# GpSimd makes the larger low part of the row operands at the beginning of the up and of the down pass, and it is made first

## Chip, core and metric

One core of a Trainium2 chip runs the whole program. The metric is the device time in microseconds, as the median of several runs; smaller is better. The engines are TensorE (PE, with its weight loads as PEld), VectorE (DVE), ScalarE (ACT), GpSimd (POOL) and the DMA queues of SP, ACT and POOL.

## The reference, cut to what matters

One step of a decoder layer for 512 prompt rows and 64 sample rows (576 rows of 2048 channels): a combined input projection, attention and a convolution branch, an output projection, then the part that matters here, an MLP with a squared ReLU, and a gated embedding:

```python
x = x + jnp.concatenate([attn, conv_y], axis=-1) @ w_out
hid = jnp.square(jax.nn.relu(rms_norm(x, g_mlp) @ w_up))     # 2048 -> 8192
x = x + hid @ w_down                                         # 8192 -> 2048
gate = jax.nn.sigmoid(rms_norm(x, g_ple) @ w_ple_gate)
x = x + (pe @ w_ple) * gate                                  # then a last rms_norm
```

## The kernel before, in words

**Precision.** All matmuls run on a rounded form of float32. A number is split into a high part (the rounded copy, made by ACT in `split_hi`, line L149) and a low part (the difference, made by DVE in `split_lo`, L152), and a product takes three matmuls: high x high (L1547), high x low (L1548), low x high (L1549).

**Tiles of the up and the down pass.** The 576 rows are two halves of 288, the channels pairs of 128-blocks. A pair of input blocks against a pair of output blocks is a 2 x 2 block product, done with seven products instead of eight: seven sums of weight blocks (`w2r`, sums in L1770 to L1772, then split into `w2h` and `w2l`) meet seven sums of row blocks. Such a set of seven row blocks, high and low, is a row operand, `xs`: 128 partitions x 2 x 7 x 288. One tile of work on PE is 21 matmuls of 288 columns, three for each of the seven products. Behind the last tile of an output pair the seven results in PSUM are combined by ACT and DVE (L1663 to L1666, L1676 to L1679); the next output pair can take a PSUM bank only when the combination has read it, L1664 first.

**Passes.** The up pass has 32 output pairs over 8 operands (k = 0 to 7), the down pass 8 output pairs over 32 operands, cut in rounds so that operands can come one after the other: the first round takes three operands for the output pairs 0 to 2, then 4, 5, 6, 7 and 8. A gate pass follows.

**Where the operands come from.** The seven sums of rows (three blocks direct, four computed, `T`) are written to DRAM by POOL's queue (`stored`, L1314 to L1316; tiles `ui` for the up pass, `di` for the down pass) and read back by POOL's queue into the low half of a slot of a ring of eight (L1470), when the slot's last reader on PE is through. Then `slot` builds the operand in the place: it takes three of the seven blocks (128 x 864), lets ACT copy the rounded high part into the high half and DVE subtract it in the low half, and then the other four (128 x 1152). Three up operands (k = 0, 1 and 7) are not read back but made directly from the sums (`split7`).

**The seams.** At the beginning of the up pass the last sums have only just been finished, so five operands (k = 2 to 6) are built within some twenty microseconds; at the beginning of the down pass eight slots change their contents while PE works on the first rounds. Later operands come one at a time.

**Order of the work.** Each engine works through its instructions in the order in which this program writes them. `Beside` keeps queues of background work (generators): behind each tile of PE it adds a credit in microseconds for DVE and steps through generators until the credit is used; a generator yields what its step costs DVE (`EL(n)` for n columns), or a negative number to be called again some tiles later. Queue 0 goes first: the sums of finished tiles, and `norm`, the row norm of the up pass: PE sums the squares (L179), DVE computes the inverse root in small steps (L181, L163 to L170, L183, L185), PE spreads it (L189), ACT copies it (L190). The builds of operands are in queue 1; before the tile that needs an operand its build is finished at once (`flush`).

Of the kernel before, what the change touches and what calls it, by code (L numbers as in the profile page):

```python
# [13 lines left out]
ALU = mybir.AluOpType  # L14
# [6 lines left out]
HR = 288  # L21
# [10 lines left out]
RING = 8  # L32
# [47 lines left out]
def f(ap):  # L80
    return ap.bitcast(F32)
# [13 lines left out]
def EL(n):  # L95

    return n / 960.0 + 0.07
# [45 lines left out]
class Kern:  # L143
# [1194 lines left out]
    def phase2(self):  # L1338
# [39 lines left out]
        def unit(i):  # L1378

            while len(units) <= i:  # L1380
                t = self.place([128, 3, 2, NR], F32R, "xs")
                units.extend(t[:, j] for j in range(3))
            return units[i]
# [75 lines left out]
        def mk(g, j):  # L1459

            h = slots[g, j] = Slot()
            if g == 3:
                h.hi, h.lo = unit(2 * j), unit(2 * j + 1)
            else:
                t = self.xslot()
                h.hi, h.lo = t[:, 0], t[:, 1]
            src = (self.up_in, self.down_in, self.x2)[g - 1][j]
            def load():
                bg.flush(fin_of[g - 1, j])
                nc.gpsimd.dma_start(f(h.lo), src)  # L1470

            if g < 3:
                load()

            def build():
                if g == 3:
                    load()
                yield -3 if g == 2 and j >= RING else -2
                if g < 3:
                    yield from self.slot(t)  # L1480
                    return
                for i in range(2):
                    gv = self.g_ple[:, 2 * j + i:2 * j + i + 1]
                    r = f(h.lo[:, i, :])
                    self.split_hi(h.hi[:, i, :], r, scale=gv)
                    nc.vector.scalar_tensor_tensor(h.lo[:, i, :], r, gv, f(h.hi[:, i, :]), ALU.mult, ALU.subtract)  # L1486
                    yield EL(NR)

            h.work = bg.add(1, build())

        quadlist = [(si, k) for si, ks in enumerate(self.orders) for k in ks]
# [11 lines left out]
        for n in range(RING, len(seq)):  # L1503
            g, j = seq[n]
# [11 lines left out]
        for t, (si, k) in enumerate(quadlist):  # L1516
            g, p, *_ = segs[si]
            ks = self.orders[si]
            n, i = len(ks), t - seg0[si]
            if prev:  # L1520
                pg, ppr, c, r, pfinal, pp_ = prev
# [10 lines left out]
            s = slots[min(g, 3), k]  # L1532
            if s.work is not None:
                bg.flush(s.work)
                s = slots[min(g, 3), k]
            bg.spend(W.prep(t + 2))
            hi, lo = W.hl.pop(t)
# [17 lines left out]
            if i == (n - 2 if g < 4 else 5) and not slow:  # L1555
                if g > 1:
                    bg.flush_all(0)
                r = pre[g](p, lastseg[g, p] == si)
# [7 lines left out]
            if i == n - 1:  # L1566
                if g > 1:
                    bg.flush_all(0)
                if slow:
                    r = pre[g](p, lastseg[g, p] == si)  # L1570
# [11 lines left out]
        pg, ppr, c, r, pfinal, p = prev  # L1582
# [61 lines left out]
            self.split_lo(l, src, h)  # L1644
            yield EL(n)

    def slot(self, s):

        hi, lo = s[:, 0], s[:, 1]
        for i, n in ((0, 3), (3, 4)):  # L1650
            r = f(lo[:, i:i + n, :])
            self.split_hi(hi[:, i:i + n, :], r)
            self.split_lo(lo[:, i:i + n, :], r, hi[:, i:i + n, :])
            yield EL(n * HR)

    def combine_head(self, pr):

# [25 lines left out]
class Slot:  # L1683
    hi = lo = work = None
# [214 lines left out]
```

## Time and profile before

| | |
|---|---|
| median of 3 runs | 2740.95 us (2735.22 to 2743.04) |
| the profiled execution | 2746.47 us, its span 2744.7 us, mean granted clock 0.991 |
| up pass on PE begins | 1043 us |
| down pass on PE begins | about 1770 us |
| builds by `slot` | 37, each with 864 and 1152 columns on ACT and on DVE |
| POOL instructions | 906, 511.0 us busy, most of it ahead of the up pass |

In the rows of the profile, a line is that of the kernel file, and a line of a helper such as L152 collects several uses, which the tile names tell apart (`xs` operands, `w2l` weights). A row of a timeline has start, duration, engine, line, operation, tiles and shapes; "x2" merges two neighbours, even of different shapes; square brackets give idle time of the engine before it and what ended it. In a wait row stand the total, the count and the longest.

### The profile page before, as it was taken

What the parts mean: (1) busy time and instruction counts of PE and PEld (TensorE: products, weight loads), DVE (VectorE), ACT (ScalarE), POOL (GpSimd) and SP (SyncE); (2) the same over time, 40 slices, a digit from 0 to 9 for tenths busy, and PEclk for the clock granted to TensorE, in tenths of its full rate; (3) what the DMA queues carried; (4) which work ended last, traced back from release to release, by engine and by line L of the source; (5) the groups of instructions that cost most, each with busy time, mean ns of one, the idle gap of its engine ahead of it and who ended that gap; (6) DMA issues with size and microseconds to landing.
All of it is one profiled execution on the core that took longest, in us unless ns stands there. A gap on an engine that the chain in (4) does not pass through costs nothing.

```text
span 2744.7 us, 56305 instructions
## 1 busy us (share of the span) xinstructions
PE 2670.7 (97%) x21873; PEld 2575.1 (94%) x21873; DVE 2043.5 (74%) x3553; ACT 1152.6 (42%) x1692; POOL 511.0 (19%) x906
## 2 busy tenths in 40 slices
PE   8999999998999999999999999999999999998997
PEld 8999999877889998999999999999999999998997
DVE  5577777645444447888888888898888888887676
ACT  4222232334443224444444444444444444444554
POOL 2188787601000000000000000100000000000110
PEclk9999999999999999999999999999999999999999
DMA  5488888898754454444444444666565656655675
GB/s 197 148 299 289 301 291 290 287 320 285 253 191 151 160 197 156 154 143 138 138 138 140 145 143 138 242 149 172 164 191 149 182 158 173 179 169 179 199 241 175
DMA packets 238382, 536.12 MB, mean 195 GB/s; under 512 B 25537, under 2 KB 26562, under 8 KB 238114
## 3 DMA queue, kind: packets, MB, share of 16 engines
q1 hardware_dynamic: 170978, 327.86, 37.7%
q0 software_dynamic: 33600, 143.70, 16.7%
q10 hardware_dynamic: 33536, 60.96, 6.9%
q8 instruction: 171, 2.80, 0.4%
q14 instruction: 97, 0.79, 0.1%
HBM read 441.47 MB, written 90.96 MB: 194 GB/s over the span
## 4 chain that ended last, share of the span: by engine, by line
PE 49%; issue 5%; DVE 3%; DMA 1%; ACT 1%; POOL 0%; DVEq 0%; ACTq 0%; POOLq 0%
PE P L1548 14%; PE P L1547 14%; PE P L1549 14%; PE P L1615 2%; PE P L1617 2%; PE P L1616 2%; DVE w2l L152 1%; DMA xs<-x 1%; ACT w2h L149 0%; DMA xs<-di 0%; DMA x<-c 0%; DVE w2r L1770 0%; DVE w2r L1771 0%; DVE w2r L1772 0%; DVE xs L1486 0%
## 5 line engine op out<-in xcount | busy, mean ns | idle before, releaser
L1547 PE MATMUL P<-xs,w2h 128*128 128x288 f32 x3584 | 1064.5, 297 | 17.0 <-DVE c L1664 8.0
L1548 PE MATMUL P<-xs,w2h 128*128 128x288 f32 x3584 | 1064.4, 297 | 4.7 <-DVE xs L152 4.7
L1549 PE MATMUL P<-xs,w2l 128*128 128x288 f32 x3584 | 1061.4, 296 | 2.8 <-DVE w2l L152 2.6
L149 ACT ACTIVATE w2h<-w2r 128x896 fp32r<-128x896 f32 (+1 forms) x632 | 556.0, 889 | 723.7 <-PE P L1548 425.6
L152 DVE TENSOR_TENSOR w2l<-w2r,w2h 128x896 fp32r<-128x896 f32 (+1 forms) x632 | 637.9, 1012 | 218.1 <-ACT w2h L149 215.6
L1547 PEld LDWEIGHTS P<-xs,w2h 128*128 128x128 f32 x3584 | 676.8, 189 | 23.6 <-DVE c L1664 11.1
L1548 PEld LDWEIGHTS P<-xs,w2h 128*128 128x128 f32 x3584 | 677.3, 189 | 7.3 <-DVE xs L152 7.0
L1549 PEld LDWEIGHTS P<-xs,w2l 128*128 128x128 f32 x3584 | 674.9, 188 | 5.1 <-DVE w2l L152 4.9
L497 PE MATMUL U<-xh,whi 128*128 128x288 f32 x1792 | 400.6, 305 | 3.6 <-ACT xh L149 2.2
L497 PE MATMUL U<-xh,wlo 128*128 128x288 f32 x1792 | 385.3, 297 | 1.4 <-DVE wlo L129 1.4
L497 PE MATMUL U<-xl,whi 128*128 128x288 f32 x1792 | 385.2, 297 | 1.6 <-DVE xl L331 1.6
L497 PEld LDWEIGHTS U<-xh,whi 128*128 128x128 f32 x1792 | 288.2, 190 | 22.5 <-issue 16.3
L123 ACT ACTIVATE whi<-wraw 128x512 fp32r<-128x512 f32 x224 | 141.2, 630 | 393.5 <-PE U L497 217.7
L497 PEld LDWEIGHTS U<-xl,whi 128*128 128x128 f32 x1792 | 289.8, 190 | 2.6 <-DVE xl L331 2.5
L497 PEld LDWEIGHTS U<-xh,wlo 128*128 128x128 f32 x1792 | 289.7, 190 | 2.2 <-DVE wlo L129 2.1
L129 DVE TENSOR_TENSOR wlo<-wraw,whi 128x512 fp32r<-128x512 f32 x224 | 160.2, 715 | 133.9 <-ACT whi L123 132.5
L1044 DVE SCALAR_TENSOR_TENSOR y<-ue,cv,y 128x512 f32<-128x512 f32 x240 | 183.8, 766 | 5.3
L1770 DVE TENSOR_TENSOR w2r<-w2r 128x512 f32<-128x512 f32 (+1 forms) x273 | 177.7, 651 | 5.2 <-DMA w2r<-in_w_down 5.2
L1045 POOL TENSOR_SCALAR cvt<-us,cv 128x64 f32<-128x64 f32 x240 | 162.8, 678 | 22.3
L1615 PE MATMUL P<-xs,w2h 128*128 128x288 f32 x512 | 151.8, 297 | 0.4 <-ACT c L1663 0.4
L1617 PE MATMUL P<-xs,w2l 128*128 128x288 f32 x512 | 151.0, 295 | 1.1 <-DVE w2l L152 1.0
L1616 PE MATMUL P<-xs,w2h 128*128 128x288 f32 x512 | 150.8, 295 | 0.0
(382 smaller groups left out, 2761.1 us busy)
## 6 DMA issues: line engine op xcount, KB each, us to landing
k<-in_cache_kv SPq DMA_DIRECT2D x256, 256.0 KB, 4.7
v<-in_cache_kv SPq DMA_DIRECT2D x256, 256.0 KB, 4.6
w2r<-in_w_up SPq DMA_DIRECT2D x127, 512.0 KB, 4.0
w2r<-in_w_down SPq DMA_DIRECT2D x112, 512.0 KB, 4.3
wraw<-in_w_main ACTq DMA_DIRECT2D x156, 256.0 KB, 4.9
xs<-di POOLq DMA_DIRECT2D x32, 1008.0 KB, 6.1
w2r<-in_w_gate SPq DMA_DIRECT2D x60, 512.0 KB, 4.6
x<-c POOLq DMA_DIRECT2D x48, 576.0 KB, 6.4
```

Source lines behind the costliest of these rows:

```text
L149: self.nc.scalar.activation(out, in_, AF.Copy, **kw)
L152: self.nc.vector.tensor_tensor(out, in_, f(hi), ALU.subtract)
L497: self.nc.tensor.matmul(u[:, r, :HR], w, x[:, r * HR:(r + 1) * HR], start=first and n == 0, stop=last and n == 2)
L1044: nc.vector.scalar_tensor_tensor(y, ue[:, j:j + NPR], w, y, ALU.mult, ALU.add)
L1045: nc.gpsimd.tensor_scalar(t, us[:, :, j:j + 8], w, None, ALU.mult)
L1547: nc.tensor.matmul(o, hi[:, ia, :], s.hi[:, ib, :], start=(i == 0), stop=False)
L1548: nc.tensor.matmul(o, hi[:, ia, :], s.lo[:, ib, :], start=False, stop=False)
L1549: nc.tensor.matmul(o, lo[:, ia, :], s.hi[:, ib, :], start=False, stop=(i == n - 1))
L1615: nc.tensor.matmul(o, hi[:, ia, :], s.hi[:, kh, rows], start=first and kh == 0, stop=False)
L1616: nc.tensor.matmul(o, hi[:, ia, :], s.lo[:, kh, rows], start=False, stop=False)
L1617: nc.tensor.matmul(o, lo[:, ia, :], s.hi[:, kh, rows], start=False, stop=last and kh == 1)
L1770: lambda: V(w[:, :, 4:6, :], w[:, :, 0:1, :].broadcast_to([128, m, 2, 128]), w[:, :, 1:3, :], ALU.add),
```

## The change

`slot` gets an argument `seam`, which is true for the five up operands that it builds and for the first eight down operands. There the part of four blocks comes ahead of the part of three. ACT makes its high part as before, but its low part is subtracted by GpSimd; and the generator yields once, with the cost of the part of three alone, where it yielded twice. Other operands are built as before. `f` reads a tile as plain float32.

```diff
                 if g < 3:
-                    yield from self.slot(t)
+                    yield from self.slot(t, g == 1 or j < RING)
                     return
...
-    def slot(self, s):
+    def slot(self, s, seam):
 
         hi, lo = s[:, 0], s[:, 1]
-        for i, n in ((0, 3), (3, 4)):
+        for i, n in ((3, 4), (0, 3)) if seam else ((0, 3), (3, 4)):
             r = f(lo[:, i:i + n, :])
             self.split_hi(hi[:, i:i + n, :], r)
-            self.split_lo(lo[:, i:i + n, :], r, hi[:, i:i + n, :])
-            yield EL(n * HR)
+            if seam and i:
+                self.nc.gpsimd.tensor_tensor(lo[:, i:i + n, :], r, f(hi[:, i:i + n, :]), ALU.subtract)
+            else:
+                self.split_lo(lo[:, i:i + n, :], r, hi[:, i:i + n, :])
+                yield EL(n * HR)
```

Three lines are added, so that lines behind it have numbers three higher in the kernel after; GpSimd's subtraction is its L1654.

On DVE at the beginning of the up pass stood, behind the direct build of operand 7 (`acc` are the squares of the rows, `w2r` the weight sums):

```order
L152 TENSOR_TENSOR xs<-xs 128x864
L152 TENSOR_TENSOR xs<-xs 128x1152
L152 TENSOR_TENSOR w2l<-w2r,w2h 128x896
L1290 TENSOR_TENSOR acc_12131<-acc_12131,sq_14258 128x576
L152 TENSOR_TENSOR xs<-xs 128x864
L152 TENSOR_TENSOR xs<-xs 128x1152
L1770 TENSOR_TENSOR w2r<-w2r 128x256
L152 TENSOR_TENSOR w2l<-w2r,w2h 128x896
```

and at the same place stands now, down to the third build and the start of the row norm:

```order
L152 TENSOR_TENSOR xs<-xs 128x864
L152 TENSOR_TENSOR w2l<-w2r,w2h 128x896
L1290 TENSOR_TENSOR acc_12131<-acc_12131,sq_14258 128x576 x2
L152 TENSOR_TENSOR xs<-xs 128x864
L1773 TENSOR_TENSOR w2r<-w2r 128x256
L152 TENSOR_TENSOR w2l<-w2r,w2h 128x896
L1774 TENSOR_TENSOR w2r<-w2r 128x128
L152 TENSOR_TENSOR xs<-xs 128x864
L1775 TENSOR_TENSOR w2r<-w2r 128x128
L152 TENSOR_TENSOR w2l<-w2r,w2h 128x896
L181 TENSOR_SCALAR rrm<-P 128x5
L163 TENSOR_SCALAR rrt<-rrm 128x5
```

The parts of 1152 columns are gone; the second accumulation has come forward, and so has the norm, whose fourteen instructions on DVE (L181 to L185) now stand between the third and the fourth build. Before, they stood behind the twelfth tile of the up pass, now PE's sum for them (L179) stands behind the fifth.

On POOL at the beginning of the down pass stood (`di_116` to `di_120` are the sums for the operands 3 to 7, `x_0` to `x_2` partial results that are added in DRAM, `di_144` the last up tile):

```order
L1470 DMA xs<-di_116 128x2016
L1470 DMA xs<-di_117 128x2016
L1470 DMA xs<-di_118 128x2016
L1470 DMA xs<-di_119 128x2016
L1470 DMA xs<-di_120 128x2016
L1363 DMA x_0_81<-c 128x1152
L1314 DMA di_144<-c 128x288
```

and now:

```order
L1470 DMA xs<-di_116 128x2016
L1654 TENSOR_TENSOR xs<-xs 128x1152
L1470 DMA xs<-di_117 128x2016
L1470 DMA xs<-di_118 128x2016
L1654 TENSOR_TENSOR xs<-xs 128x1152
L1470 DMA xs<-di_119 128x2016
L1470 DMA xs<-di_120 128x2016
L1654 TENSOR_TENSOR xs<-xs 128x1152
L1363 DMA x_0_81<-c 128x1152
L1654 TENSOR_TENSOR xs<-xs 128x1152
L1314 DMA di_144<-c 128x288
```

Loads and stores of POOL's queue now stand behind subtractions; the eight of the down pass are the four shown and four more among the stores that follow. At the up pass the five stand together, behind the last load and ahead of the first store of the pass.

## The prediction

> **What bounds the kernel now.** I read the busy times first, then a table of stretches around the two places where the change acts, the waits of TensorE, and last the timeline of VectorE there. On the page TensorE (PE) is busy almost throughout, so the most that any change can win is the small idle time in it.
>
> ```profile
> PE 2670.7 (97%) x21873; PEld 2575.1 (94%) x21873; DVE 2043.5 (74%) x3553; ACT 1152.6 (42%) x1692; POOL 511.0 (19%) x906
> ```
>
> The table of stretches (length, then busy time of PE, PEld, DVE, ACT and POOL, then the granted clock) cuts out the beginning of the up pass (from 1043 us) and of the down pass (from about 1770 us):
>
> ```profile
> 1050.00:1073.00 23.00, 19.02 (x129) 16.99 (x127) 22.06 (x28) 15.98 (x19) 0.00 (x0) 1.00 0.65 237
> 1073.00:1120.00 47.00, 46.53 (x342) 45.27 (x343) 40.76 (x75) 20.45 (x26) 3.25 (x6) 1.00 0.42 128
> 1740.00:1760.00 20.00, 20.00 (x152) 20.00 (x152) 16.68 (x28) 10.90 (x14) 3.23 (x6) 1.00 0.67 223
> 1760.00:1784.00 24.00, 20.12 (x134) 19.06 (x134) 21.94 (x34) 11.08 (x15) 2.68 (x6) 0.93 0.91 350
> 1784.00:1807.00 23.00, 19.91 (x142) 18.70 (x142) 19.87 (x35) 10.56 (x14) 3.49 (x5) 1.00 0.65 171
> 1807.00:1834.00 27.00, 25.65 (x189) 25.05 (x188) 26.16 (x41) 14.56 (x18) 1.72 (x2) 1.00 0.61 143
> 1834.00:1890.00 56.00, 55.96 (x418) 55.83 (x419) 50.23 (x77) 27.72 (x32) 4.26 (x6) 1.00 0.65 182
> ```
>
> In the first and in the fourth to sixth row PE is idle for 3.98, 3.88, 3.09 and 1.35 us while DVE has hardly any idle time (0.94, 2.06, 3.13 and 0.84 us). Ahead of and behind them PE is full. So VectorE bounds the two seams, and only there. The waits of PE over the whole program name the same engine, by the low parts of the operands (xs) and by the combination that frees a PSUM bank (c):
>
> ```profile
> PE P L1547 <- DVE c L1664: 8.0, 11, 1.3
> PE P L1548 <- DVE xs L152: 4.7, 8, 1.1
> ```
>
> **What the change takes from VectorE.** Thirteen operands are built in the seams, five for the up pass and eight for the down pass. Here are three builds of the up seam in VectorE's timeline, an accumulation and a weight split (w2l) between them, and the combination behind the seam; and the groups of the two forms:
>
> ```profile
> 1050.66 2.42 DVE L152 TENSOR_TENSOR xs<-xs 128x864 fp32r<-128x864 f32 x2 [0.35 <-ACT xs L149]
> 1053.99 0.75 DVE L1290 TENSOR_TENSOR acc<-acc,sq 128x576 f32<-128x576 f32 x1
> 1054.66 2.32 DVE L152 TENSOR_TENSOR xs<-xs 128x864 fp32r<-128x864 f32 x2
> 1064.72 1.08 DVE L152 TENSOR_TENSOR w2l<-w2r,w2h 128x896 fp32r<-128x896 f32 x1
> 1066.06 2.32 DVE L152 TENSOR_TENSOR xs<-xs 128x864 fp32r<-128x864 f32 x2
> 1072.68 0.45 DVE L1664 TENSOR_TENSOR c<-c,P 128x288 f32<-128x288 f32 x1
> L152 DVE TENSOR_TENSOR xs<-xs 128x1152 fp32r<-128x1152 f32 x37 | 50.1, 1355 | 0.0
> L152 DVE TENSOR_TENSOR xs<-xs 128x864 fp32r<-128x864 f32 x37 | 39.0, 1054 | 4.1 <-ACT xs L149 3.9
> ```
>
> A build holds VectorE for 2.32 us; without its larger part 1.05 us are left, so 1.27 us go from each.
>
> **What GpSimd needs for it.** The trace has no subtraction of this size on POOL. It has two smaller ones with two inputs, at moments when VectorE did nothing: 64 columns (shortest, median, longest ns of seven) and 128 columns.
>
> ```profile
> L1056 POOL TENSOR_TENSOR ysum<-ysum,ys x7: 322/323/325, 223.9 to 535.9; 128x64 f32<-128x64 f32 x7
> 62.70 0.46 POOL L663 TENSOR_TENSOR suf<-suf,L 128x128 f32<-128x128 f32 x1
> ```
>
> 64 more columns cost 0.137 us, 2.14 ns each; 1152 columns are 0.46 + 1024 x 0.00214 = 2.65 us, my value. The low bound is VectorE's own 1.27 us; the high one scales with the 0.99 us that the 128 columns take beside a busy VectorE (below), 2.65 x 0.99 / 0.46 = 5.7 us. I stay with the undisturbed pair, since what the high row holds more is waiting, which I count by itself. The Trainium skill (GPSIMD Engine Reference, section 3.1) gives 4497 ns for such an addition of 2048 columns; in proportion that is an estimate of 2.53 us, and the sum below would be 1.4 us smaller by it.
>
> **What POOL does to VectorE meanwhile.** This decides the sign. Two moments of the trace, POOL and DVE side by side:
>
> ```profile
> 58.90 0.17 DVE L168 TENSOR_TENSOR rrt<-rrs 128x5 f32<-128x5 f32 x1
> 58.92 0.47 POOL L663 TENSOR_TENSOR suf<-suf,L 128x128 f32<-128x128 f32 x1
> 59.10 0.31 DVE L169 SCALAR_TENSOR_TENSOR rrt<-rrt,rrm 128x5 f32<-128x5 f32 x1
> 60.54 0.69 DVE L183 TENSOR_TENSOR xraw<-ident,rrs 128x512 f32<-128x512 f32 x1
> 60.56 0.99 POOL L663 TENSOR_TENSOR suf<-suf,L 128x128 f32<-128x128 f32 x1
> ```
>
> The DVE instruction that started at 59.10 does the same tiny work as its neighbour of 0.17 us, but takes 0.31 us and ends at 59.41, just behind the POOL instruction's end at 59.39. In the second pair POOL is the one that waits: its 0.46 us become 0.99, the missing half being VectorE's 0.69. So the two engines exclude each other when both read two tensors from SBUF, in both directions, and each seems to wait for the other's whole instruction. The rows show it for a POOL instruction of 0.46 us only; whether VectorE also stands still for 2.65 us is the open step. The Trainium skill (SBUF — State Buffer, "Who interferes with whom") says so for any length: the second to start fully blocks until the first has finished. If that holds, moving 1.27 us off VectorE closes VectorE for 2.65 us: 1.38 us worse for each operand.
>
> **The up seam, summed on VectorE from 1050.66 to 1072.68.** Removed: 5 x 1.27 = 6.35. Added: 5 x 2.65 = 13.25 of closed time. One accumulation (L1290) moves in from behind the seam: 0.67. And, since the first part no longer counts against the scheduler's credit, the whole norm chain moves in between the third and the fourth build. Its rows in the trace of before:
>
> ```profile
> 1084.61 0.17 DVE L181 TENSOR_SCALAR rrm<-P 128x5 f32<-128x5 f32 x1 [1.56 <-PE P L179]
> 1087.64 0.25 DVE L185 TENSOR_SCALAR dg<-ident,rrs 128x64 f32<-128x64 f32 x1
> ```
>
> It runs 3.2 us from 1084.61 to the end of the second row, behind a wait of 1.56 us for PE. There it stood beside a full PE and cost nothing; in the seam its 3.2 us and half of the wait, 0.8 us, lie on the path. Of the same step, PE's few small matmuls (L179, L189) and ACT's two copies (L190) come earlier too, in a stretch where both wait for VectorE anyway: nothing. VectorE's idle 0.94 us cover as much. Sum: 13.25 - 6.35 + 0.67 + 3.2 + 0.8 - 0.94 = 10.6; the 0.47 us that PE idles from 1073 to 1120, partly at that chain, come back: **+10.1 us**.
>
> **The down seam.** Marks in VectorE's timeline: the first two builds, the second part of the third, the fifth and the sixth, and the combination that frees PE's banks at the start and at the end:
>
> ```profile
> 1760.43 2.32 DVE L152 TENSOR_TENSOR xs<-xs 128x864 fp32r<-128x864 f32 x2
> 1767.61 2.32 DVE L152 TENSOR_TENSOR xs<-xs 128x864 fp32r<-128x864 f32 x2
> 1771.06 0.45 DVE L1664 TENSOR_TENSOR c<-c,P 128x288 f32<-128x288 f32 x1
> 1779.55 1.35 DVE L152 TENSOR_TENSOR xs<-xs 128x1152 fp32r<-128x1152 f32 x1
> 1821.54 2.32 DVE L152 TENSOR_TENSOR xs<-xs 128x864 fp32r<-128x864 f32 x2
> 1829.96 2.32 DVE L152 TENSOR_TENSOR xs<-xs 128x864 fp32r<-128x864 f32 x2
> 1833.54 0.45 DVE L1664 TENSOR_TENSOR c<-c,P 128x288 f32<-128x288 f32 x1
> ```
>
> Between 1760.43 and 1833.54 stood the builds of six operands; in the new order seven POOL parts and the smaller part of the seventh operand fall there. Removed 6 x 1.27 = 7.6; added 7 x 2.65 = 18.55, and 1.05: +12.0. VectorE's idle time there is 6.03 us; I let half of it cover, 3.0, because the rest waits for PE or ACT in places that move along. The combinations read PSUM and one tensor of SBUF, which I take not to be excluded; one POOL part lies beside one, 2.0 us. That leaves **+7.0 us**. The third operand's larger part comes earlier than 1779.55, which is part of the cover, not a further gain. The eighth operand is built where VectorE has 5.8 us to spare in 56: nothing.
>
> Costed at nothing: on POOL, the loads of the down operands 4 to 7 and the stores of the last up tile and of x1 now queue behind POOL parts that wait for ACT; each is one part later, 2.65 us, and the fifth operand is not built before 1821.54, fifty microseconds behind the last up tile. If that cover were gone, 2.65 us would be the price. ACT does the same two copies in the other order.
>
> **Sum.** The profiled execution took 2746.47 us; 2746.5 + 10.1 + 7.0 = 2763.6. The median of the runs, 2740.95, lies 5.5 lower, so **2758 us**.
>
> **Rivals.** *VectorE is not closed for the whole instruction*, only for short pieces of it. For it: no POOL instruction over 0.99 us that reads two tensors is in the trace; against it: 59.41 against 59.39. Then VectorE is 1.27 us lighter per build; up, 3.98 us of idle PE come back less 2.5 for the norm chain, 1.5; down, some 6 of 8.3: 2741 - 7.5 = 2733.5. It decides if VectorE loses less than 1.27 us per part. Chance 0.08, three quarters of it below the bound of faster. *The closed time finds cover*: all of it in the down seam (6.0 us idle and six combinations), and in the up seam the POOL parts cost only what they remove, so that the norm chain and the accumulation remain, about 4: 2745. Against it: 0.94 us of idle time in the up seam. Chance 0.09. *The clock falls as well.* In the down seam, PE idled before these rows,
>
> ```profile
> 1779.41 0.40 PE L1547 MATMUL P<-xs,w2h 128*128 128x288 f32 x1 [1.98 <-ACT xs L149]
> 1781.60 0.44 PE L1547 MATMUL P<-xs,w2h 128*128 128x288 f32 x1
> ```
>
> and the stretch has a clock of 0.93: 24 x 0.07 / 0.5 = 3.4 us at half speed, 1.7 us lost. My stalls are longer than those; four such losses, where VectorE doesn't hide them, give 2758 + 7 = 2765. Chance 0.13.
>
> **The numbers.** A measurement tells 0.3%, 8 us, from no change. Forecast 0.70; slower with the clock 0.83; same 0.09 + 0.02 = 0.11; faster 0.06. The range: down by a POOL part without its fixed share, 1152 x 2.14 ns = 2.47 us (12 x 0.18 = 2.2), the other half of the idle cover (3.0) and half of the norm chain with its wait (2.0), to 2751, and on to 2746, most of the way to the second rival; up by no cover under a combination (2) and four clock losses (7), about 2768. What is left out holds the first rival, the rest of the second and little of the third, some 0.18.
>
> **What would show it.** POOL L1654 near 2.65 us, or over it by a DVE instruction that it waits for; DVE instructions in the seams (w2l at 1.08, xs at 1.05, w2r) two to three times as long, ending just behind a POOL part; the stretch of the up seam some 10 us longer, PE idle there about 14 instead of 4, the down seam 7. I am wrong if w2l keeps 1.08 us beside L1654, or if POOL parts take under 1.5 us.

## The result, and the profile after

The changed kernel takes **2764.19 us** as the median of four runs (2759.30 to 2775.75), the kernel before 2738.09 beside it (four runs, 2728.60 to 2743.04): 1.0086 times as long, 95% interval 1.0064 to 1.0107. The forecast was 2758, range 2746 to 2768. The profiled execution took 2760.86 us (its span 2759.1, mean granted clock 0.984).

The page's busy times of the kernel after:

```profile
PE 2668.7 (97%) x21873; PEld 2575.8 (93%) x21873; DVE 2058.7 (75%) x3540; ACT 1154.0 (42%) x1692; POOL 548.3 (20%) x919
```

VectorE has 13 instructions fewer and is busy 15.2 us longer: what was taken from it came back as waiting inside its instructions. Stretches of the seams (length, busy PE, PEld, DVE, ACT, POOL, then the clock), first of the kernel before, then of the kernel after:

```profile
1040.00:1100.00 60.00, 55.84 (x401) 53.03 (x401) 51.19 (x83) 30.18 (x38) 3.16 (x6) 1.00 0.52 175
1770.00:1834.00 64.00, 55.67 (x387) 52.83 (x386) 58.01 (x96) 30.43 (x39) 5.74 (x8) 0.97 0.68 194
1834.00:1890.00 56.00, 55.96 (x418) 55.83 (x419) 50.23 (x77) 27.72 (x32) 4.26 (x6) 1.00 0.65 182
```

```profile
1040.00:1100.00 60.00, 46.15 (x305) 44.60 (x304) 48.64 (x65) 27.66 (x33) 20.03 (x14) 0.86 0.44 156
1770.00:1834.00 64.00, 52.76 (x342) 51.13 (x342) 58.12 (x86) 28.85 (x37) 17.31 (x14) 0.87 0.64 186
1834.00:1890.00 56.00, 52.62 (x379) 51.69 (x378) 49.57 (x72) 22.80 (x28) 9.38 (x7) 0.97 0.48 119
```

In the same lengths PE does 96, 45 and 39 instructions less, its clock falls to 0.86, 0.87 and 0.97, and POOL is busy 17, 12 and 5 us longer. In the third row of before PE was full; now it idles for 3.4 us. PE's waits for the low parts and for the combination, over the whole program after:

```profile
PE P L1548 <- DVE xs L152: 16.0, 4, 7.6
PE P L1549 <- DVE w2l L152: 8.3, 9, 1.8
PE P L1547 <- DVE c L1667: 7.2, 8, 2.1
PE P L1547 <- ACT c L1666: 4.6, 2, 3.7
```

The wait for `xs` was 4.7 us in eight pieces and is 16.0 us in four; that for `w2l` was 2.6 us in four and is 8.3 in nine. The wait for the combination on VectorE (L1667, L1664 before) did not grow in sum, 7.2 us after 8.0, but its longest did, 2.1 after 1.3, and that on ScalarE (L1666) was 2.0 us in three pieces. GpSimd's subtraction by itself (shortest, median, longest ns):

```profile
L1654 POOL TENSOR_TENSOR xs<-xs x13: 2615/2970/3466, 1049.9 to 1850.7; 128x1152 fp32r<-128x1152 f32 x13
```

The undisturbed ones take 2.62 to 2.65 us, the others up to one VectorE instruction more. The open step of the prediction stands in the timelines of POOL and DVE in the up seam:

```profile
1049.90 2.64 POOL L1654 TENSOR_TENSOR xs<-xs 128x1152 fp32r<-128x1152 f32 x1 [4.19 <-ACT xs L149]
1050.66 2.79 DVE L152 TENSOR_TENSOR xs<-xs 128x864 fp32r<-128x864 f32 x1 [1.40 <-ACT xs L149]
1052.60 3.41 POOL L1654 TENSOR_TENSOR xs<-xs 128x1152 fp32r<-128x1152 f32 x1
1053.38 3.58 DVE L152 TENSOR_TENSOR w2l<-w2r,w2h 128x896 fp32r<-128x896 f32 x1
1055.97 3.47 POOL L1654 TENSOR_TENSOR xs<-xs 128x1152 fp32r<-128x1152 f32 x1
1056.88 3.18 DVE L1290 TENSOR_TENSOR acc<-acc,sq 128x576 f32<-128x576 f32 x1
...
1070.24 0.17 DVE L181 TENSOR_SCALAR rrm<-P 128x5 f32<-128x5 f32 x1 [2.42 <-PE P L179]
1071.22 2.65 POOL L1654 TENSOR_TENSOR xs<-xs 128x1152 fp32r<-128x1152 f32 x1 [8.70 <-ACT xs L149]
1071.26 2.65 DVE L170 SCALAR_TENSOR_TENSOR rrs<-rrt,rrs 128x5 f32<-128x5 f32 x1
```

Read the ends: POOL 1052.54, DVE 1053.45; POOL 1056.01, DVE 1056.96; POOL 1059.44, DVE 1060.06. Each VectorE instruction ends 0.6 to 1.0 us behind a POOL part, which is about its own undisturbed time, and each POOL part ends 2.5 to 2.6 us behind a VectorE instruction. So the two take strict turns, one whole instruction each. A `w2l` that takes 1.08 us alone takes 3.58, and in the last row one of the norm's steps on 128 x 5 numbers lasts 2.65 us instead of 0.17. The Trainium skill (SBUF — State Buffer, "Who interferes with whom") says that the one that comes second is blocked for the whole instruction; these rows agree, at 2.65 us. Two rows of the down seam below do not fit it by their recorded starts; there the measurement decides (last section).

PE in the same seam, at full and at half clock (in brackets the wait ahead of the row):

```profile
1054.01 0.30 PE L1548 MATMUL P<-xs,w2h 128*128 128x288 f32 x1
1054.15 0.30 PE L1549 MATMUL P<-xs,w2l 128*128 128x288 f32 x1
...
1064.16 0.61 PE L1548 MATMUL P<-xs,w2h 128*128 128x288 f32 x1 [7.60 <-DVE xs L152]
1064.57 0.44 PE L1549 MATMUL P<-xs,w2l 128*128 128x288 f32 x1
1064.81 0.44 PE L1547 MATMUL P<-xs,w2h 128*128 128x288 f32 x1
```

Behind the wait of 7.60 us matmuls follow each other every 0.24 us instead of 0.14. The trace's record of the clock has it at half for 10.24 us from 1058.6 and 6.83 us from 1075.7 (before: never in this seam), and in the down seam for four stretches of 20.5 us together (before: one of 3.41).

In the down seam:

```profile
1777.91 0.45 DVE L1680 TENSOR_TENSOR t<-P,t 128x288 f32<-128x288 f32 x1
1777.97 2.68 POOL L1654 TENSOR_TENSOR xs<-xs 128x1152 fp32r<-128x1152 f32 x1 [1.41 <-ACT xs L149]
1778.28 0.45 DVE L1681 TENSOR_TENSOR c<-c,P 128x288 f32<-128x288 f32 x1
1778.76 2.50 DVE L1682 TENSOR_TENSOR c<-c,t 128x576 f32<-128x576 f32 x1
...
1817.58 0.86 POOL L1363 DMA_DIRECT2D x<-c  x1 [5.66 <-DVE c L1682]
1817.80 4.30 DVE L152 TENSOR_TENSOR w2l<-w2r,w2h 128x896 fp32r<-128x896 f32 x1
1818.16 2.98 POOL L1654 TENSOR_TENSOR xs<-xs 128x1152 fp32r<-128x1152 f32 x1
...
1850.27 4.31 DVE L152 TENSOR_TENSOR w2l<-w2r,w2h 128x896 fp32r<-128x896 f32 x1
1850.66 2.97 POOL L1654 TENSOR_TENSOR xs<-xs 128x1152 fp32r<-128x1152 f32 x1
```

The steps of the combination that read PSUM and one tensor of SBUF (L1680, L1681) keep their 0.45 us beside the POOL part, as the prediction assumed. The step behind them (L1682), with both inputs in SBUF, takes 2.50 us; elsewhere in this trace it takes 0.76. The last pair belongs to the eighth operand, which was costed at nothing.

**Where the time went.** To place it I take from each trace the start of every 21st of the 10752 large matmuls of the up and the down pass, that is of each tile, numbered through. "Up seam" is from tile 0 to tile 16, "up pass" from there to tile 240, "down seam" from tile 248 to tile 290.

| us, profiled executions | before | after | difference |
|---|---|---|---|
| up seam | 53.28 | 66.18 | +12.90 |
| up pass behind it (224 tiles) | 628.56 | 619.73 | -8.83 |
| down seam | 130.50 | 143.49 | +12.99 |
| all else | 1932.37 | 1929.70 | -2.67 |
| span | 2744.71 | 2759.10 | +14.39 |

The seams lose 25.9 us. That the two profiled spans differ by 14.4 only is due to the rest, and above all to the up pass: of its 8.8 us, 1.4 lie in the tiles 16 to 29, where PE before still waited for `w2l` and did the norm's last matmuls, and 7.5 are a shorter time for each tile, which is taken up at the end. The medians differ by 26.1 us, with an interval of 17.5 to 29.3, so that their closeness to 25.9 doesn't show whether the other runs of the change had the short tiles too.

### The profile page after: what moved, and what is told of

Same layout as the page of the kernel before. It is cut to its first block, busy times and chain, and to the rows that moved or that the text cites. A ratio compares the mean times of both kernels' runs of the same rounds, so it can differ in the third digit from the quotient of the medians.

```text
span 2759.1 us, 56320 instructions
## 1 busy us (share of the span) xinstructions
PE 2668.7 (97%) x21873; PEld 2575.8 (93%) x21873; DVE 2058.7 (75%) x3540; ACT 1154.0 (42%) x1692; POOL 548.3 (20%) x919
## 5 line engine op out<-in xcount | busy, mean ns | idle before, releaser
L152 DVE TENSOR_TENSOR w2l<-w2r,w2h 128x896 fp32r<-128x896 f32 (+1 forms) x632 | 647.3, 1026 | 214.1 <-ACT w2h L149 212.6
L1548 PEld LDWEIGHTS P<-xs,w2h 128*128 128x128 f32 x3584 | 681.3, 190 | 17.3 <-DVE xs L152 17.1
```

Source lines behind the costliest of these rows:

```text
L152: self.nc.vector.tensor_tensor(out, in_, f(hi), ALU.subtract)
L1548: nc.tensor.matmul(o, hi[:, ia, :], s.lo[:, ib, :], start=False, stop=False)
```

## The experiments

Two theories stood against each other. *Closed*: POOL's reads exclude VectorE, 2.65 us for each part against 1.27 saved. *Order and queue*: what costs is the new order (larger part first, one credit, the norm in the seam) and that the part arrives late from POOL, behind its queue. Each kernel's stretches, as above, with its median and that of the kernel before on the same chip:

| kernel | ratio (95%) | medians | up seam | up pass | down seam |
|---|---|---|---|---|---|
| before | | | 53.28 | 628.56 | 130.50 |
| the change | 1.0086 (1.0064 to 1.0107) | 2764.19 / 2738.09 | 66.18 | 619.73 | 143.49 |
| up_only | 1.0027 (1.0009 to 1.0045) | 2748.87 / 2742.32 | 65.95 | 619.73 | 130.60 |
| down_only | 1.0047 (1.0024 to 1.0069) | 2756.58 / 2742.32 | 53.19 | 628.55 | 144.90 |
| credit_kept | 1.0058 (1.0035 to 1.0081) | 2761.37 / 2742.32 | 60.25 | 628.55 | 144.59 |
| vector_same_order | 1.0007 (0.9991 to 1.0024) | 2745.94 / 2742.32 | 55.82 | 627.20 | 132.12 |
| pool_writes_only | 0.9974 (0.9952 to 0.9996) | 2730.96 / 2738.95 | 55.61 | 619.73 | 125.04 |
| pool_reads_one | 1.0039 (1.0019 to 1.0058) | 2751.04 / 2738.95 | 60.85 | 619.73 | 138.45 |
| pool_pieces | 1.0073 (1.0051 to 1.0096) | 2759.67 / 2738.95 | 62.06 | 619.73 | 148.49 |
| clock_kept | 1.0069 (1.0044 to 1.0095) | 2757.42 / 2738.95 | 62.62 | 619.73 | 143.81 |
| last_two | 1.0026 (1.0001 to 1.0050) | 2744.53 / 2740.72 | 53.26 | 628.56 | 132.87 |
| vector_larger_first | 1.0006 (0.9987 to 1.0025) | 2739.90 / 2740.72 | 53.46 | 621.53 | 131.31 |

The stretches come from one profiled execution each; in those of down_only and vector_same_order 26 and 6 matmul records are missing, so that their figures can be off by 0.2 us. All diffs are against the changed kernel, with most lines around them left out.

**One seam at a time**, up_only and down_only:

```diff
-                    yield from self.slot(t, g == 1 or j < RING)
+                    yield from self.slot(t, g == 1)                    # up_only
+                    yield from self.slot(t, g == 2 and j < RING)       # down_only
```

> The change in the up seam alone. Measured from the first tile of the up pass on PE to the seventeenth, before took 53.3 us and the changed kernel 66.2. Closed VectorE: 66 us here, the down seam (from the 249th to the 291st tile, 130.5 us before, 143.5 changed) as before, the whole 10 to 13 us longer than before (ratio 1.004 to 1.005). If the loss came from POOL's queue (late loads and stores of the down pass), both stretches stay as before and the ratio is 1.000.

> The change in the down seam alone. Closed VectorE: the up stretch 53 us as before, the down stretch 143 us, the whole about 13 us longer (ratio 1.005). If the two seams hang together (one loss, passed on), the down stretch stays near 131 us.

Each seam loses as much alone as in the whole change (up +12.7 of 12.9; down +14.4 against 13.0), and the other one stays as before. The two add up; nothing is carried from one to the other through POOL's queue. The median of down_only is 14.3 us above before, as expected; that of up_only is only 6.5 above, less than the 10 to 13 expected (see the end).

**The work on POOL with the norm where it was**, credit_kept: the part on POOL is counted in the credit too, so that the norm stays behind the twelfth tile.

```diff
                 self.nc.gpsimd.tensor_tensor(lo[:, i:i + n, :], r, f(hi[:, i:i + n, :]), ALU.subtract)
+                yield EL(n * HR)
```

> GpSimd makes the parts as in the change, but the generator also yields for them, with the cost that VectorE's part had, so that the row norm stays where it was (behind the twelfth tile). Closed VectorE: in the up stretch the 5 x (2.65 - 1.27) = 7 us of the parts remain, 60 us; the down stretch 141 to 144 us; the whole +18 to +20 us (ratio 1.007). If the moved norm were the main loss of the up seam, its stretch falls to 54 us.

**The order with the work on VectorE**, vector_same_order: everything as in the change, the subtraction on DVE.

```diff
-                self.nc.gpsimd.tensor_tensor(lo[:, i:i + n, :], r, f(hi[:, i:i + n, :]), ALU.subtract)
+                self.split_lo(lo[:, i:i + n, :], r, hi[:, i:i + n, :])
```

> All as in the change (larger part first, one yield, norm moved forward), but VectorE makes the larger parts itself. Closed VectorE: only the norm and the accumulation remain as a loss in the up seam, 4 to 5 us: 57 to 58 us; the down stretch 128 to 131 us, since the third operand's larger part comes earlier; the whole +1 to +4 us (ratio 1.000 to 1.0015). If the order and the credit were the cause and not GpSimd, both stretches are as long as in the changed kernel, 66 and 143 us.

These two split the up seam. Order and norm alone cost 2.5 us there and 1.6 in the down seam, both about one microsecond beside their bounds (1.4 of the 2.5 come back in the up pass, 627.20 after 628.56). The five POOL parts, with the norm where it was, cost 60.25 - 53.28 = 7.0 us, which is 5 x (2.65 - 1.27) = 6.9. In the down seam they cost 14.1, where 8 x 1.38 is 11.0; that is 0.6 us more than expected. Two pairs of the table differ in nothing but the engine that subtracts: the change and vector_same_order (10.4 us in the up seam, 11.4 in the down seam), and credit_kept and vector_larger_first, the last of the experiments (6.8 and 13.3). So order and credit are not the cause. In the up seam 12.9 is 3.4 us more than 2.5 + 7.0: the norm's steps meet the POOL parts (the row of 2.65 us above). How much of each is shut-out time and how much the clock can't be read from these two: credit_kept too ran at half clock for 10.2 us in its up seam.

**What on POOL does the harm.** Three kernels put other work of about the same length in the part's place: three fills that read nothing (pool_writes_only), two copies that read one tensor (pool_reads_one), and the subtraction in four pieces of 288 columns (pool_pieces). In the first two the low half isn't the difference.

```diff
-                self.nc.gpsimd.tensor_tensor(lo[:, i:i + n, :], r, f(hi[:, i:i + n, :]), ALU.subtract)
+                for _ in range(3):                                                  # pool_writes_only
+                    self.nc.gpsimd.memset(f(lo[:, i:i + n, :]), 0.0)
+                for _ in range(2):                                                  # pool_reads_one
+                    self.nc.gpsimd.tensor_copy(lo[:, i:i + n, :], r)
+                for k in range(i, i + n):                                           # pool_pieces
+                    self.nc.gpsimd.tensor_tensor(lo[:, k, :], f(lo[:, k, :]), f(hi[:, k, :]), ALU.subtract)
```

> In place of the subtraction, GpSimd fills the larger low part with zeros three times (the low part of these blocks is left out of the computation): about as long as the subtraction, three times 1.0 us by the rate of the 2560-column fill, but it reads nothing. If what closes VectorE is the reading by both, VectorE's instructions keep their durations (w2l 1.08 us) and it is 1.27 us lighter per operand: the up stretch 51 to 55 us, the down stretch 126 to 131 us, the whole between 0 and 6 us shorter than before (ratio 0.998 to 1.000). If the loss comes from a part being ready late, from POOL's queue, or from any POOL instruction, the stretches stay near 66 and 143 us.

The fills and VectorE's weight splits in the up seam (1040 to 1120 us), in the groups of pool_writes_only, and one such split beside ten fills in a row, in its timelines:

```profile
L1655 POOL MEMSET xs<- 128x1152 f32 x39 | 42.2, 1087 | 14.7 <-ACT xs L149 13.2
L152 DVE TENSOR_TENSOR w2l<-w2r,w2h 128x896 fp32r<-128x896 f32 x23 | 25.0, 1088 | 6.4 <-ACT w2h L149 6.4
1051.27 10.76 POOL L1655 MEMSET xs<- 128x1152 f32 x10 [4.16 <-ACT xs L149]
1053.03 1.09 DVE L152 TENSOR_TENSOR w2l<-w2r,w2h 128x896 fp32r<-128x896 f32 x1
```

POOL is occupied for 3 x 1.09 = 3.26 us per operand, longer than by the subtraction, and so the low part is ready later, but `w2l` keeps its 1.09 us. So neither POOL's queue nor a late part is the cause. The down seam becomes 5.5 us shorter than before, 1.0 beyond the expected bound: this is what taking 1.27 us per operand off VectorE would bring there if POOL left it alone. The up seam, with the norm in it, was 55.6, 0.6 us beyond its bound. The whole is faster than before, 0.9974 (0.9952 to 0.9996), by 8.0 us, where up to 6 were expected and the two seams give 3.1; in the profiled execution the up pass behind them gives 8.8 more. The Trainium skill (SBUF — State Buffer, "Who interferes with whom") says that a VectorE instruction with two SBUF inputs collides with a GpSimd instruction that reads SBUF and not with one that only writes; these rows agree.

> In place of the subtraction, GpSimd copies the part onto itself twice (one tensor read, the subtraction left out); a copy of 1152 columns should take 1.0 to 1.5 us. If a read of one tensor closes VectorE as well, w2l beside it takes 2 us and more and the stretches lie between those of before and of the change by the length of the copies: 58 to 64 us up, 135 to 142 us down. If only two tensors on both sides collide, as for the zeros: 51 to 55 and 126 to 131 us.

Reads of one tensor close VectorE as well: `w2l` takes 2.03 us, and both seams come out inside the bounds expected for this. In the timeline of pool_reads_one, and its copies over the whole program:

```profile
1055.13 2.03 DVE L152 TENSOR_TENSOR w2l<-w2r,w2h 128x896 fp32r<-128x896 f32 x1
1057.09 3.31 DVE L1290 TENSOR_TENSOR acc<-acc,sq 128x576 f32<-128x576 f32 x2
```

```profile
L1655 POOL CAST xs<-xs x26: 1147/1484/2057, 1053.2 to 1845.8; 128x1152 fp32r<-128x1152 f32 x26
```

> GpSimd makes the larger low part in four instructions of 288 columns, 0.8 us each by the rate of the trace, instead of one of 2.65. Exclusion by whole instructions: no VectorE instruction waits for more than 0.8 to 0.9 us at a time (2.65 and more in the change), VectorE gets one instruction in after each piece, and the closed time grows to 4 x 0.8 = 3.2 us per operand, so that the stretches are as long as in the change or up to 5 us longer (66 to 71 and 143 to 149 us). If the exclusion were by short slices, nothing changes in the single waits beside that in the change.

```profile
L1655 POOL TENSOR_TENSOR xs<-xs x52: 781/982/1709, 1050.5 to 1852.5; 128x288 fp32r<-128x288 f32 x52
```

Four pieces are 4 x 0.78 = 3.1 us undisturbed, 4.3 at their mean of 1.08. Single VectorE instructions wait less, but the down seam is 148.5, longer than with whole parts; the up seam, 62.1, fell below the 66 that I had expected at the least. Smaller pieces do not help the sum of the seams, 26.8 us after 25.9.

**The clock**, clock_kept: 36 matmuls more ahead of tile 4 and 18 ahead of tile 6 of the up pass keep PE at work while it waits for VectorE; their products are added to a result in the up pass.

```diff
+                for _ in range({4: 36, 6: 18}.get(t, 0)):
+                    nc.tensor.matmul(pr[3][:, :HR], last[0][:, 3, :], last[1].hi[:, 1, :], start=False, stop=False)
+                last = hi, s
```

> The changed kernel with PE kept busy in the up seam: 36 matmuls of the tile before are repeated ahead of the fifth tile and 18 ahead of the seventh (they add to one product, whose result is not the reference's), where PE stood idle for 7.8 and 4.0 us and its clock fell to half for 17 us. If the clock costs about 5 us of the up stretch, as the rows after those stalls say (tile 7 starts 2.8 us later than its operand allows), it falls from 66 to 60 to 62 us, with a clock of 1.00 in the table of stretches. If VectorE hides the half clock, the stretch stays at 65 to 67 us. The down stretch stays at 143 us.

The stretch from 1040 to 1110 us, of the change and of clock_kept:

```profile
1040.00:1110.00 70.00, 56.15 (x381) 54.60 (x380) 57.28 (x80) 32.19 (x39) 20.03 (x14) 0.88 0.46 159
```

```profile
1040.00:1110.00 70.00, 65.04 (x462) 63.82 (x461) 59.24 (x84) 33.08 (x40) 20.17 (x14) 0.95 0.48 164
```

The clock rises from 0.88 to 0.95, not to the expected 1.00 (half for 6.8 us instead of 17.1), and the up seam shrinks from 66.18 to 62.62, 0.6 us above its bound: the lower clock costs **3.6 us** of the up seam, and I take it to be more, since some of it was left. The norm's wait for PE falls with it, from 2.42 to 1.02 us. The down seam is as in the change.

**The end of the down seam**, last_two: only the seventh and the eighth operand of the down pass go to POOL, the ones that I had costed at least.

```diff
-                    yield from self.slot(t, g == 1 or j < RING)
+                    yield from self.slot(t, g == 2 and j in (6, 7))
```

> The change for the seventh and the eighth operand of the down pass alone, all others as before; there PE was full before and VectorE had 5.8 us to spare in 56. If spare time on average is cover, as the prediction had it for the eighth operand, the down stretch stays at 130 to 131 us and the ratio at 1.000. If a closed VectorE costs at once what it delays, because the low parts of the weights are made only two tiles ahead of their use, each part costs PE 1 to 3 us: 133 to 136 us (ratio 1.001 to 1.002).

The timelines around the eighth operand's part, and the wait of PE from 1820 to 1920 us:

```profile
1853.54 4.29 DVE L152 TENSOR_TENSOR w2l<-w2r,w2h 128x896 fp32r<-128x896 f32 x1
1853.92 2.95 POOL L1654 TENSOR_TENSOR xs<-xs 128x1152 fp32r<-128x1152 f32 x1
```

```profile
PE P L1549 <- DVE w2l L152: 2.2, 1, 2.2
```

The seventh costs nothing. The eighth makes the down seam 2.4 us longer, nearly all of it in one wait of 2.2 us, between the two stretches that were expected: the instruction that POOL shut out is a weight split that PE needs at once. So VectorE's 5.8 us of idle time in that stretch were no cover.

**A version for use**, vector_larger_first: the new order of the two parts, both on VectorE, both counted.

```diff
-                self.nc.gpsimd.tensor_tensor(lo[:, i:i + n, :], r, f(hi[:, i:i + n, :]), ALU.subtract)
+                self.split_lo(lo[:, i:i + n, :], r, hi[:, i:i + n, :])
+                yield EL(n * HR)
```

> VectorE makes both parts as before, with both yields, but the larger part first: what is left of the change without GpSimd and without the moved norm. It could beat both kernels if the third down operand's larger part, which comes late before (1779.55), was worth its stall of some 4 us: the down stretch 127 to 130 us, the up stretch 53 us, ratio 0.998 to 1.000. If what counts there is VectorE's total work, both stretches stay within a microsecond of before (53.3 and 130.5 us), ratio 1.000.

Both stretches stay within a microsecond of before, the second of the two expectations, and the whole can't be told from the kernel before. No version that computes the reference was shown to be faster than that.

## Why the prediction was right, and where it was wrong

- **Direction and size.** Slower, 2764 against a forecast of 2758: in the range. The sum was +17.1 us; the seams and the medians say 26. It was 9 us too small; that the forecast missed by 6 only is luck, since the median of the kernel before is now 2.9 us below the one that it started from. The range held because its upper end had room for the two terms that fell short, the cover and the clock.
- **What POOL needs.** 2.65 us from the two small shapes; measured 2.62 to 2.65 undisturbed. The Trainium skill's figure (GPSIMD Engine Reference, section 3.1), in proportion an estimate of 2.53, is 0.1 us low.
- **The open step.** VectorE is closed for the whole instruction: shown by the turns in the timeline and by pool_writes_only, where POOL is as occupied but reads nothing. That kernel is the first rival's world: its down seam is 5.5 us shorter, where the rival had some 6; its up seam is 2.3 longer, where the rival had 1.5 less.
- **PSUM.** Combinations that read PSUM and one SBUF tensor are not excluded: right. But the cover that was built on it was too large, since the step L1682 behind them is.
- **Up seam, +10.1; measured +12.9.** PE idled 13.9 us there (60 less 46.15), where the prediction said about 14. The parts measured 7.0 (summed 6.9) and the order 2.5 (summed 4.7, less 0.94 idle time and 0.47 that was to come back; 1.4 did, behind tile 16). The mis-sized term is their meeting: the norm's wait for PE was costed at 0.8 us, half of 1.56, and lasted 2.42, with PE at half clock up to 1068.9, just ahead of it (1.02 in clock_kept); one of its steps stood for 2.65 us.
- **Down seam, +7.0; measured +13.0, and +14.1 and +14.4 in two other kernels.** The failed step is the cover: 3.0 us of idle time, 2.0 under a combination, and "the eighth operand: nothing". Without it, 8 x 1.38 = 11.0 and 1.6 for the order make 12.6. Against the kernel before, the down pass was 3.0 us late at tile 256, 1.1 at tile 260, 9.3 at tile 270 and 13.0 at tile 278: each part that met a busy VectorE came through. The third operand's earlier larger part did give back about two of the first three microseconds.
- **The clock.** The rival "the clock falls as well" (0.13) happened together with the forecast, in both seams; its time, 2765, is the nearest to the measured one. Its price in the up seam was 3.6 us, against 7 for four losses. In the down seam, with 20.5 us at half clock, it wasn't taken apart, so what I put down to the missing cover there may hold some of it; how the loss of 13 us divides between the two stays open.
- **Costed at nothing.** POOL's later loads and stores: right, by the two seams that add up and by pool_writes_only, whose POOL is occupied longer in the same order.
- **The other side.** "The closed time finds cover" (2745): wrong in both seams.

## What to carry to other kernels

Moving an elementwise instruction with SBUF inputs from VectorE to GpSimd did not take it off VectorE here, where both were at work: price it by GpSimd's duration less VectorE's, here 2.65 - 1.27 = 1.38 us each, and expect that this is paid in full on a stretch that VectorE bounds, as in both seams here. Idle time of the closed engine is cover only if the instruction that gets shut out isn't the next one waited for; look at which instruction stands there, not at the sum of the idle time. Where stalls of the tensor engine grow (here from at most 1.0 us in the up seam to 7.6, with 10.2 us at half clock), put the half clock into the sum from the start.

## What was not expected of the hardware

**VectorE can lose although it started first.** At 1817.80 and 1850.27 a `w2l` began 0.4 us ahead of the POOL part and still ended about 1 us behind it, 4.3 us for 1.08. In both, and in last_two at 1853.54, the `w2l` began 0.2 us into a store's issue on POOL (L1363), and the part stood right behind that issue. So a part can cost VectorE 3.2 us. The issue alone doesn't do it, as two rows of the kernel before show:

```profile
1786.40 0.93 POOL L1363 DMA_DIRECT2D x<-c  x1 [15.59 <-DVE c L1679]
1786.61 1.08 DVE L152 TENSOR_TENSOR w2l<-w2r,w2h 128x896 fp32r<-128x896 f32 x1
```

Why the two together do it is open.

**Fills collide with some VectorE instructions.** In the timeline of pool_writes_only, two steps of the norm that read one tensor, 0.17 us in the kernel before:

```profile
1062.67 0.51 DVE L163 TENSOR_SCALAR rrt<-rrm 128x5 int32<-128x5 int32 x1
1063.20 2.09 DVE L164 TENSOR_SCALAR rrs<-rrt 128x5 int32<-128x5 int32 x1
```

They wait for one fill and for two, while subtractions with two inputs beside them do not.

**Two speeds of the same pass.** 500 us of the up pass, the same code in both, of before and of after:

```profile
1120.00:1620.00 500.00, 500.00 (x3750) 499.73 (x3749) 427.72 (x674) 233.27 (x268) 35.55 (x66) 1.00 0.45 141
```

```profile
1120.00:1620.00 500.00, 500.00 (x3797) 500.00 (x3796) 431.50 (x680) 235.83 (x271) 35.98 (x67) 1.00 0.46 143
```

PE is full and at full clock in both, yet does 47 instructions more in the second: 2.767 us for a tile instead of 2.800, kept through the whole pass, 7.5 us for its 224 tiles. Six of the seven profiled kernels that work on POOL in the up seam had the short one (credit_kept the long one); of the five without such work, vector_larger_first had it and four not. Where the profile had it and the work was on POOL, the medians lie up to 6 us below the sum of the seams (up_only +6.5 against +12.8), though not in the change itself (26.1 against 25.9). What sets the speed is open.
